# A gated RMS norm inside one fused layer on Trainium2: the row sums and the spread of the reciprocal root, by transposes instead of fp32 matmuls

## The chip, the cores and the metric

The kernel runs on one core of one Trainium2 chip. The metric is the device time of one execution in microseconds (us); the time before is 1612.79 us, the median of three runs that lie between 1611.87 and 1614.87.

Engine names are those of the profile: PE is the matrix engine's matmuls, PEld its weight loads, DVE the vector engine, ACT the scalar engine (ScalarE), POOL is GpSimd, SP the engine that only issues DMAs. "Column" below means a block of 128 sequence positions, which is what one 128 x 128 instruction handles.

## The reference, cut to what matters

The reference computes one layer: a combined input projection of x (1024 positions, width 2048), sparse attention on one half of the mixing width, a Mamba-2 (SSD) mixer on the other half, one output projection and a layer norm. The change touches the last step of the SSD mixer only, the gated norm:

```
g = (y * silu(z)).reshape(bsz, seq, G, SSD_WIDTH // G)          # G = 4 groups of 256 channels
g = g * rsqrt(mean(square(g), axis=-1, keepdims=True) + RMS_EPS)  # RMS_EPS = 1e-5
return g.reshape(bsz, seq, SSD_WIDTH) * norm_w
```

For each position and each of four groups, the mean of 256 squares is taken over the channels, and its reciprocal root multiplies those 256 channels.

## The kernel before

All large products are done in three fp32r passes: an operand is split into a rounded part (tiles `wh`, `xh`, made by ACT) and the rest (tiles `wl`, `xl`, made by DVE, now and then by POOL), and PE accumulates high x high, high x low and low x high in a `pj` bank of PSUM. The sequence is worked in two halves of 512 positions (`h`); channels lie on the partitions, positions along the row. First come the input projections, whose stream of `pj` matmuls goes on to the end of the attention and SSD work; that work is slipped in between them as tasks. Then come the output projection and the layer norm.

Nothing is issued in the order in which the Python text stands. The tasks record instructions (class `Flow`, with a table of engine costs in `Sim.cost`), and then class `Order` lays the recorded instructions out once more: it gives PE, at each point, the first block within a window of 100 whose inputs are there, and each other engine the ready instruction with the earliest due time. Each engine then runs its own queue strictly in that order and waits at the head of it. So a change of an instruction's cost or engine can shift the order of everything behind it, and slots of the pools go to other tiles. All instructions are emitted by one line, L611, so the profile's groups are told apart by tile names: `u`, `xh`, `xl`, `s` are work tiles in SBUF (freed operand slots serve as work tiles too), `sm` are small ones of four columns, `a`, `o`, `pj` are PSUM banks, `c` is the constant tile `c3` whose first third is the identity, `mhalf` holds -0.5. The letter `o` as an input is the constant `o256`, 1/256 in each partition.

The gate is the task `t_gate` (L2380 to L2442). It takes one half, one group and either one chunk pair of 256 positions (two columns) or, if the group's gates are still held in the work tiles, a whole half of 512 (four columns); `wide` says which. In the program before, all 16 gates are of two columns. Its steps:

- L2405 to L2412: multiply by the gate, square on ACT, add the two squared halves of the 256 channels (`zs`, first part: 128 partitions by 256 positions).
- L2413 to L2418: per column one fp32 matmul with the squares as weights and `o256` as the one moving column. The sum over the partitions, divided by 256, lands in one column of an `a` bank, with the positions on the partitions.
- L2420: DVE adds EPS while it moves the two columns to `sm`.
- L2423: POOL raises them to -0.5 (`pow` with `mhalf`).
- L2424 to L2427: per column one fp32 matmul with the `sm` column, broadcast along the row, as weights and the identity as moving operand, which spreads the 128 roots over all partitions, along the row.
- L2428 to L2430: DVE multiplies the two halves of the channels by norm weight and root; then the tile is stored to a scratch (`mx`, `my` in the profile) which the output projection reads.

The helper `fl.mm` issues a matmul, `fl.tr` a transpose against the identity, `fl.act` an activation, `fl.ts`, `fl.stt` and `fl.two` element-wise work.

Of the kernel before, what the change touches and what calls it, by code (L numbers as in the profile page):

```python
# [13 lines left out]
AF = mybir.ActivationFunctionType  # L14
ALU = mybir.AluOpType
# [4 lines left out]
P = 128  # L20
# [3 lines left out]
EPS = 1e-5  # L24
# [843 lines left out]
class Layer:  # L868
# [687 lines left out]
    def consts(self):  # L1556
        a, nc = self.a, self.nc
        c3 = self.const("c3", [P, 3, P])
        nc.sync.dma_start(c3, a["c3"])
        self.ident, self.tri, self.ones = c3[:, 0], c3[:, 1], c3[:, 2]  # L1560
        self.fl.ident = self.ident
        self.ps, self.pso, self.res, self.mv, self.lnB = {}, {}, {}, {}, {}
        self.cw = self.const("cw", [P, 16, 5])
        nc.sync.dma_start(self.cw, a["cw"])
        self.dn = self.const("dn", [P, 2, 8])
        nc.sync.dma_start(self.dn, a["dn"])
        self.hp = self.const("hp", [P, 2, 16])
        nc.sync.dma_start(self.hp, a["hp"].partition_broadcast(P))
        self.mhalf = self.const("mhalf", [P, 4])
        nc.gpsimd.memset(self.mhalf, -0.5)  # L1570
        self.m01 = self.const("m01", [P, 384], BF)
        nc.gpsimd.memset(self.m01, 0.0)
        nc.gpsimd.memset(self.m01[0:64, 64:128], HIDE)
        nc.gpsimd.memset(self.m01[0:64, 320:384], HIDE)
        self.zero16 = self.const("zero16", [P, 2], BF)
        nc.gpsimd.memset(self.zero16, 0.0)
        self.o256 = self.const("o256", [P, 1])
        nc.gpsimd.memset(self.o256, 1.0 / 256.0)
        self.carry = self.const("carry", [P, 16, 3])
        nc.gpsimd.memset(self.carry, 0.0)  # L1580
        self.nea = self.const("nea", [P, 16])
        for h in range(2):
            setattr(self, f"sd{h}", {k: self.const(f"{k}{h}", [P, 64]) for k in ("wsc", "dt", "ac", "ddt", "cdec")})
# [796 lines left out]
    def t_gate(self, h, g, cps, xy=None, zz=None):  # L2380

        fl, nc = self.fl, self.nc
        w = 256 * len(cps)
        cols = slice(256 * cps[0], 256 * cps[0] + w)
        held = [self.zg[h, g, j] for j in range(2)]
        wide = held[0][0] is not None
        evs = () if xy is not None else tuple(self.ev_y[h, g, cp] for cp in cps)
        yield Need("", us=(xy is None) * (1 if w == 256 else 2) + (zz is None and not wide), ev=evs + tuple(e for _, e in held))
        if wide:
            zs = [x for x, _ in held]  # L2390
            xs = [fl.new("us", [P, HALF]) for _ in range(2)]
            for j in range(2):
                fl.dma(xs[j], self.y_sc[h, g][j])
            tiles = xs + zs
            part = lambda t, j: t[j]
        else:
            if zz is None:
                zz = fl.new("us", [P, 2, 256])
                fl.dma(zz, self.zs_sc[h, g][:, :, cols].rearrange("j p s -> p j s"))
            if xy is None:  # L2400
                xy = fl.new("us", [P, 2, 256])
                fl.dma(xy, self.y_sc[h, g][:, :, cols].rearrange("j p s -> p j s"))
            xs, zs, tiles = [xy], [zz], [xy, zz]
            part = lambda t, j: t[0][:, j]
        yield Need("G", late=2500.0)  # L2405
        for x, z in zip(xs, zs):
            fl.two(x, x, z, ALU.mult)
        yield Need("A")
        for x, z in zip(xs, zs):
            fl.act(z, x, AF.Square)  # L2410
        yield Need("G")
        fl.two(part(zs, 0), part(zs, 0), part(zs, 1), ALU.add)  # L2412
        yield Need("P", a=1, sm=1)  # L2413
        sm = fl.new("sm", [P, 4])
        nq = w // P
        b = fl.new("a", [P, 512])
        for c in range(nq):
            fl.mm(b[:, c:c + 1], part(zs, 0)[:, c * P:(c + 1) * P], self.o256)  # L2418
        yield Need("V")
        fl.ts(sm[:, 0:nq], b[:, 0:nq], EPS, None, ALU.add)  # L2420
        fl.free(b)
        yield Need("G")
        nc.gpsimd.tensor_tensor(out=sm[:, 0:nq], in0=sm[:, 0:nq], in1=self.mhalf[:, 0:nq], op=ALU.pow)  # L2423
        yield Need("P", a=1)  # L2424
        b = fl.new("a", [P, 512])
        for c in range(nq):
            fl.mm(b[:, c * P:(c + 1) * P], sm[:, c:c + 1].to_broadcast([P, P]), self.ident)  # L2427
        yield Need("V")  # L2428
        for j in range(2):
            fl.stt(part(xs, j), part(xs, j), self.dn[:, 1, 2 * g + j:2 * g + j + 1], b[:, 0:w], ALU.mult, ALU.mult)  # L2430
        fl.free(b, sm)
        yield Need()
        n = self.gated[h, g] = self.gated.get((h, g), 0) + len(cps)
        if wide:
            for j in range(2):
                fl.dma(self.mixed[h][8 + 2 * g + j], xs[j])
        else:
            fl.dma(self.mixed2[h][g][:, :, cols].rearrange("j p s -> p j s"), xy)
        if n == 2:
            for j in range(2):  # L2440
                fl.signal(self.ev_mix[h, 8 + 2 * g + j])
        fl.free(*tiles)  # L2442
# [212 lines left out]
```

## Time and profile before

| what | value |
|---|---|
| median of the three runs | 1612.79 us |
| the profiled execution's own time | 1613.98 us |
| its span, first to last instruction | 1612.2 us |
| mean granted PE clock | 0.997 |
| gates | 16, the first sum at 643.8 us, the last spread at 1400.4 us |

The profile is of one execution. Busy shares are over the whole span; a group of instructions is named by what it writes and reads. "Idle before" is the idle time of an engine just before the instructions of a group, with what ended it. A matmul's duration in the profile includes its pipeline, so what a matmul costs PE is read from the distance between starts, not from its length.

### The profile page before, as it was taken

What the parts mean: (1) busy time and instruction counts of PE and PEld (TensorE: products, weight loads), DVE (VectorE), ACT (ScalarE), POOL (GpSimd) and SP (SyncE); (2) the same over time, 40 slices, a digit from 0 to 9 for tenths busy, and PEclk for the clock granted to TensorE, in tenths of its full rate; (3) what the DMA queues carried; (4) which work ended last, traced back from release to release, by engine and by line L of the source; (5) the groups of instructions that cost most, each with busy time, mean ns of one, the idle gap of its engine ahead of it and who ended that gap; (6) DMA issues with size and microseconds to landing.
All of it is one profiled execution on the core that took longest, in us unless ns stands there. A gap on an engine that the chain in (4) does not pass through costs nothing. (4 is left out here: it accounts for less than half of the span.)

```text
span 1612.2 us, 24012 instructions
## 1 busy us (share of the span) xinstructions
PE 1592.8 (99%) x7996; PEld 1338.9 (83%) x7996; DVE 1327.0 (82%) x2437; ACT 1005.9 (62%) x1774; POOL 213.3 (13%) x212
## 2 busy tenths in 40 slices
PE   9999999999999999999999999999999999999997
PEld 7888898888788888888888888888878888888885
DVE  6989999988689976879676787867888788559998
ACT  5565666758989799785443557768775754332420
POOL 0000110200101110302021313222120101000100
PEclk9999999999999999999999999999999999999999
DMA  9657956999779877687665675589899889847554
GB/s 344 218 190 259 335 182 237 340 402 379 270 239 307 298 264 239 224 302 271 211 236 179 219 229 160 158 278 294 266 298 347 287 298 358 282 151 241 183 179 131
DMA packets 192637, 414.49 MB, mean 257 GB/s; under 512 B 19712, under 2 KB 56192, under 8 KB 192512
## 3 DMA queue, kind: packets, MB, share of 16 engines
q1 hardware_dynamic: 192080, 412.56, 75.6%
q8 instruction: 63, 1.03, 0.3%
q14 instruction: 62, 0.51, 0.1%
q10 hardware_dynamic: 432, 0.39, 0.1%
HBM read 308.94 MB, written 103.94 MB: 256 GB/s over the span
## 5 line engine op out<-in xcount | busy, mean ns | idle before, releaser
L611 PE MATMUL pj<-xh,wh 128*128 128x512 f32 (+1 forms) x1496 | 581.5, 389 | 0.0
L611 PE MATMUL pj<-xh,wl 128*128 128x512 f32 (+1 forms) x1496 | 571.2, 382 | 0.1
L611 PE MATMUL pj<-xl,wh 128*128 128x512 f32 (+1 forms) x1496 | 570.8, 382 | 0.0
L611 ACT ACTIVATE wh<-wr 128x1024 fp32r<-128x1024 f32 (+2 forms) x241 | 248.8, 1033 | 210.9 <-PE pj L611 185.9
L611 DVE TENSOR_TENSOR wl<-wr,wh 128x1024 fp32r<-128x1024 f32 (+2 forms) x236 | 283.4, 1201 | 63.8 <-ACT wh L611 61.3
L611 PEld LDWEIGHTS pj<-xh,wl 128*128 128x128 f32 x1496 | 281.5, 188 | 56.1 <-DVE wl L611 0.5
L611 PEld LDWEIGHTS pj<-xh,wh 128*128 128x128 f32 x1496 | 281.6, 188 | 50.8 <-issue 1.5
L611 PEld LDWEIGHTS pj<-xl,wh 128*128 128x128 f32 x1496 | 282.0, 189 | 49.0
L611 PE MATMUL a<-u,u 128*128 128x512 f32 (+3 forms) x742 | 172.6, 345 | 0.8 <-DVE u L611 0.5
L611 DVE TENSOR_TENSOR u<-u,u 128x512 f32<-128x512 f32 (+7 forms) x208 | 135.4, 661 | 15.0 <-ACT u L611 5.0
L611 PEld LDWEIGHTS a<-u,u 128*128 128x128 f32 x742 | 124.4, 190 | 19.8 <-DVE u L611 0.9
L611 ACT ACTIVATE u<-s,sm 128x768 bf16<-128x768 f32 (+7 forms) x132 | 129.0, 978 | 11.4 <-DVE sm L611 9.4
L611 PE MATMUL pj<-wh,xh 128*128 128x512 f32 x334 | 133.9, 401 | 0.0
L611 PE MATMUL pj<-wh,xl 128*128 128x512 f32 x334 | 130.5, 391 | 0.0
L611 PE MATMUL pj<-wl,xh 128*128 128x512 f32 x334 | 130.3, 390 | 0.0
L611 DVE TENSOR_TENSOR wr<-wr,wr 128x1024 f32<-128x1024 f32 (+1 forms) x83 | 102.9, 1241 | 24.1 <-DMA wr<-wt 23.3
L611 ACT ACTIVATE u<-u 128x512 f32<-128x512 f32 (+4 forms) x147 | 81.1, 558 | 57.2 <-DVE u L611 42.5
L611 ACT ACTIVATE a<-a 128x512 f32<-128x512 f32 (+3 forms) x160 | 78.0, 504 | 54.4 <-PE a L611 52.8
L611 DVE TENSOR_TENSOR u<-pj,u 128x512 f32<-128x512 f32 (+1 forms) x112 | 74.4, 665 | 21.7 <-PE pj L611 17.8
L611 POOL TENSOR_SCALAR s<-s,sm 128x640 f32<-128x640 f32 (+7 forms) x64 | 62.8, 992 | 193.8 <-DVE sm L611 153.8
L611 ACT ACTIVATE u<-a 128x512 fp32r<-128x512 f32 (+4 forms) x114 | 52.4, 477 | 44.1 <-PE a L611 40.5
L611 ACT ACT_TABLE_LOAD x57 | 73.1, 1283 | 10.7 <-issue 5.9
(258 smaller groups left out, 2214.9 us busy)
## 6 DMA issues: line engine op xcount, KB each, us to landing
wr<-wt SPq DMA_DIRECT2D x187, 512.0 KB, 4.9
u<-u SPq DMA_DIRECT2D x110, 256.0 KB, 4.5
wr<-t SPq DMA_DIRECT2D x44, 512.0 KB, 5.2
u<-wo SPq DMA_DIRECT2D x64, 256.0 KB, 4.5
ts<-u SPq DMA_DIRECT2D x64, 256.0 KB, 4.2
wr<-ts SPq DMA_DIRECT2D x32, 512.0 KB, 4.5
s<-xt SPq DMA_DIRECT2D x25, 512.0 KB, 6.1
t<-wr SPq DMA_DIRECT2D x22, 512.0 KB, 4.9
```

Of the source, the lines that this page charges most:

```text
L611: getattr(engines[x.eng], x.op)(*[real(v) for v in x.args], **{k: real(v) for k, v in x.kw.items()})
```

## The change

The matmuls for the sum are replaced by transposes of the squares: positions come to lie on the partitions and channels along the row of a PSUM bank. ACT then reads each column's 128 x 128 block with `Identity`, a scale of 1/256 and a bias tile `eps` holding EPS/128, and its accumulator adds up the row: 128 x EPS/128 + sum/256 is the mean plus EPS. The written block goes to the second part of `zs`, which nobody reads any more. The DVE instruction that added EPS is gone. The spread is a transpose of the broadcast column in place of a matmul with the identity.

```diff
@@ consts
-        self.o256 = self.const("o256", [P, 1])
-        nc.gpsimd.memset(self.o256, 1.0 / 256.0)
+        self.eps = self.const("eps", [P, 1])
+        nc.gpsimd.memset(self.eps, EPS / 128)
@@ t_gate
         for c in range(nq):
-            fl.mm(b[:, c:c + 1], part(zs, 0)[:, c * P:(c + 1) * P], self.o256)
-        yield Need("V")
-        fl.ts(sm[:, 0:nq], b[:, 0:nq], EPS, None, ALU.add)
+            fl.tr(b[:, c * P:(c + 1) * P], part(zs, 0)[:, c * P:(c + 1) * P])
+        yield Need("A")
+        for c in range(nq):
+            fl.act(part(zs, 1)[:, c * P:(c + 1) * P], b[:, c * P:(c + 1) * P], AF.Identity, bias=self.eps, scale=1.0 / 256,
+                   accum_out=sm[:, c:c + 1])
         fl.free(b)
         yield Need("G")
         nc.gpsimd.tensor_tensor(out=sm[:, 0:nq], in0=sm[:, 0:nq], in1=self.mhalf[:, 0:nq], op=ALU.pow)
         yield Need("P", a=1)
         b = fl.new("a", [P, 512])
         for c in range(nq):
-            fl.mm(b[:, c * P:(c + 1) * P], sm[:, c:c + 1].to_broadcast([P, P]), self.ident)
+            fl.tr(b[:, c * P:(c + 1) * P], sm[:, c:c + 1].to_broadcast([P, P]))
```

The planner lays the program out anew. In the changed program there are 15 gates, 14 of two columns and one of four, so still 32 columns. The orders of the instructions differ from shortly before the first gate on; up to there they are the same.

The first place is PE's queue at the first gate, where both programs still stand alike; `a_6711` before and `a_6713` now is the bank of the sum, `u_6604` the tile of squares. Before:

```order
L611 MATMUL pj_6559<-xh_5626,wl_6570 128x512
L611 MATMUL a_6711<-o_136,u_6604 128x1 x2
L611 MATMUL a_6717<-u_6103,u_6324 128x128
L611 MATMUL a_6717<-u_6045,u_6324 128x128
L611 MATMUL a_6717<-u_6103,u_6324 128x128
```

and now:

```order
L611 MATMUL pj_6559<-xh_5626,wl_6570 128x512
L611 MATMUL a_6713<-c_318,u_6604 128x128 x2
L611 MATMUL a_6716<-u_6105,u_6328 128x128
L611 MATMUL a_6716<-u_6046,u_6328 128x128
L611 MATMUL a_6716<-u_6105,u_6328 128x128
```

The two fp32 matmuls with one moving column have become two transposes in the same place. A row of this order is an instruction as the program issues it.

The second place is the queue of the engine that takes the sum out of PSUM, at a gate in the thick of the last input projections. Before it is DVE's; `sm_12302<-a_12294` is the sum, `wl` and `wr` are weights being split or added for the stream of projections, `dt` and `ddt` scale tiles of the SSD scan:

```order
L611 TENSOR_TENSOR wl_12265<-wr_11926,wh_12254 128x1024
L611 TENSOR_TENSOR wr_12059<-wr_12059,wr_12089 128x1024
L611 TENSOR_TENSOR u_12232<-a_12277,dt_1859 128x256
L611 TENSOR_TENSOR u_12235<-a_12277,ddt_2809 128x256
L611 TENSOR_TENSOR wr_12146<-wr_12146,wr_12229 128x1024
L611 TENSOR_SCALAR sm_12302<-a_12294 128x2
L611 TENSOR_TENSOR u_11817<-u_11817,u_12107 128x512
```

Now it is ACT's; this is the gate of four columns, `sm_13030` its sums and `wh` weights being rounded:

```order
L611 ACTIVATE wh_12973<-wr_12701 128x1024
L611 ACTIVATE u_12912<-u_12912 128x512
L611 ACTIVATE wh_13010<-wr_12794 128x1024
L611 ACTIVATE u_12959<-u_12959 128x512
L611 ACTIVATE u_12354,sm_13030<-a_13021,eps 128x128 x4
L611 ACT_TABLE_LOAD
L611 ACTIVATE u_13066<-s_2425_12256 64x512 x2
```

The step has left DVE's queue, where it stood behind splits and additions of weights, for ACT's, where it stands behind roundings of weights. The number of table loads on ACT is 57 in both programs.

## The prediction

> **What bounds the kernel now.** I read the page's head first: which engine is full, and whether at full clock.
>
> ```profile
> span 1612.2 us, 24012 instructions
> PE 1592.8 (99%) x7996; PEld 1338.9 (83%) x7996; DVE 1327.0 (82%) x2437; ACT 1005.9 (62%) x1774; POOL 213.3 (13%) x212
> PEclk9999999999999999999999999999999999999999
> ```
>
> PE is busy 1592.8 of 1612.2 us. Only 19.4 us are idle, so what PE no longer has to issue comes off the end, unless a new wait takes its place. The view of waits says what PE waited for:
>
> ```profile
> PE a L611 <- POOL sm L611: 2.9, 1, 2.9
> PE a L611 <- DVE u L611: 2.1, 3, 0.8
> ```
>
> The longest wait belongs to the gate itself: one spread matmul, reading `sm` from POOL, came 2.9 us late. The table by stages shows where the gates stand (640 to 1400 us) and what else is loaded there:
>
> ```profile
> 640.00:900.00 260.00, 259.44 (x1408) 222.25 (x1407) 202.37 (x421) 150.03 (x279) 52.63 (x42) 1.00 0.70 236
> 900.00:1100.00 200.00, 199.08 (x1069) 169.74 (x1067) 155.86 (x301) 137.84 (x259) 57.76 (x69) 1.00 0.67 215
> 1100.00:1400.00 300.00, 296.90 (x1587) 247.85 (x1586) 239.10 (x408) 188.63 (x309) 38.27 (x32) 0.99 0.92 309
> 1560.00:1613.00 53.00, 40.92 (x181) 33.57 (x179) 46.21 (x76) 0.00 (x0) 3.92 (x4) 0.94 0.39 125
> ```
>
> The columns are length, busy PE, PEld, DVE, ACT and POOL, granted clock, DMA share, GB/s. In the three gate stages ACT is busy 150, 138 and 189 us of 260, 200 and 300 (58, 69 and 63%), DVE 78, 78 and 80%. PE is the bound; ACT has the most room of the engines that feed it.
>
> **The change part by part.** First, what PE issues. The groups of the gate's matmuls, and of the transposes that the kernel has elsewhere:
>
> ```profile
> L611 PE MATMUL a<-c,s 128*128 128x128 f32 x288 | 42.1, 272 | 0.0
> L611 PE MATMUL a<-c,sm 128*128 128x128 f32 x64 | 10.1, 281 | 3.1 <-POOL sm L611 2.9
> L611 PE MATMUL a<-o,u 128*128 128x1 f32 x52 | 6.6, 231 | 0.0
> L611 PE MATMUL a<-o,xh 128*128 128x1 f32 x8 | 1.0, 229 | 0.0
> L611 PE MATMUL a<-o,s 128*128 128x1 f32 x4 | 0.5, 228 | 0.0
> ```
>
> The program issues 32 sums and 32 spreads, but the trace has 64 of each (52 + 8 + 4, and 64): an fp32 matmul runs as two passes. The transposes, mostly `a<-c,s`, stand as often in the trace as the program issues them, 408 in all: one pass each. So 64 passes of 128 go.
>
> What a pass costs is in the distance between starts. PE's timeline at one sum, at one spread and at one pair of transposes, each between projections:
>
> ```profile
> 1315.09 0.50 PE L611 MATMUL a<-o,xh 128*128 128x1 f32 x4
> 1315.45 0.48 PE L611 MATMUL pj<-wh,xh 128*128 128x512 f32 x1
> 1315.77 0.39 PE L611 MATMUL pj<-wl,xh 128*128 128x512 f32 x1
> 1316.00 0.39 PE L611 MATMUL pj<-wh,xl 128*128 128x512 f32 x1
> ```
> ```profile
> 1321.35 0.61 PE L611 MATMUL a<-c,sm 128*128 128x128 f32 x4
> 1321.71 0.48 PE L611 MATMUL pj<-wh,xh 128*128 128x512 f32 x1
> 1322.03 0.39 PE L611 MATMUL pj<-wl,xh 128*128 128x512 f32 x1
> ```
> ```profile
> 773.51 0.38 PE L611 MATMUL a<-c,s 128*128 128x128 f32 x2
> 773.65 0.48 PE L611 MATMUL pj<-xh,wh 128*128 128x512 f32 x1
> 773.96 0.40 PE L611 MATMUL pj<-xl,wh 128*128 128x512 f32 x1
> ```
>
> A projection matmul starts 0.23 us after the one before it (1315.77 to 1316.00), but the first one behind a small block takes 0.32: part of the cost of the block falls on its follower, so I count to the start of the second follower. The sum: 1315.77 - 1315.09 = 0.68, less one projection step of 0.23, is 0.45 us. The spread: 1322.03 - 1321.35 = 0.68, again 0.45. Two transposes: 773.96 - 773.51 = 0.45, less 0.23, is 0.22. Each block saves 0.23 us; two blocks at each of 16 gates make 32 x 0.23 = 7.4 us. That one gate now has four columns changes nothing, since 32 columns stay. By busy time instead, 64 + 64 passes take 6.6 + 1.0 + 0.5 + 10.1 = 18.2 us and 64 transposes 64 x 42.1/288 = 9.4, which saves 8.8; but these lengths overlap, so I take 7.4.
>
> Second, the step that takes the sum out of PSUM. DVE did it in one short instruction, and POOL's power waits for it. At the gate with the long wait, DVE's timeline and then POOL's:
>
> ```profile
> 1165.71 1.22 DVE L611 TENSOR_TENSOR wr<-wr,wr 128x1024 f32<-128x1024 f32 x1
> ...
> 1167.51 1.21 DVE L611 TENSOR_TENSOR wr<-wr,wr 128x1024 f32<-128x1024 f32 x1
> 1168.65 0.15 DVE L611 TENSOR_SCALAR sm<-a 128x2 f32<-128x2 f32 x1
> 1168.72 1.28 DVE L611 TENSOR_TENSOR u<-u,u 128x512 f32<-128x512 f32 x2
> ```
> ```profile
> 1168.87 2.82 POOL L611 TENSOR_TENSOR sm<-sm,mhalf 128x2 f32<-128x2 f32 x1 [19.31 <-DVE sm L611]
> ```
>
> The small step stood behind additions of weights until 1168.65, and then the power took 2.82 us beside two-input work on DVE, against a median of 718 ns:
>
> ```profile
> L611 POOL TENSOR_TENSOR sm<-sm,mhalf x16: 688/718/2817, 644.6 to 1398.0; 128x2 f32<-128x2 f32 x16
> L611 DVE TENSOR_SCALAR sm<-a x16: 148/153/159, 644.3 to 1397.7; 128x2 f32<-128x2 f32 x16
> ```
>
> The change takes 16 x 0.15 = 2.5 us off DVE, which is beside PE's work and counts nothing by itself, and takes the step out of that queue: 2.9 us of PE's waiting was there. The Trainium skill, SBUF — State Buffer, section "SBUF: two separate sides", has DVE and GpSimd exclude each other for a whole instruction on a shared port pair; the 2.82 us agree, and by that rule the power stays as exposed as before, since it stays on POOL.
>
> Third, what ACT gets: 32 activations of 128 x 128 from PSUM, each with a read of the accumulator. No row has just this form; the nearest are:
>
> ```profile
> L611 ACT ACTIVATE wh<-wr 128x1024 fp32r<-128x1024 f32 x232 | 244.6, 1054 | 208.6 <-PE pj L611 185.9 <-issue 21.1 <-ACT a L611 1.1
> L611 ACT ACTIVATE s<-s,ac 128x128 f32<-128x128 f32 x128 | 40.9, 390 | 0.4
> L611 ACT ACTIVATION_READ_ACCUMULATOR s<-s,sm 128x1 f32 x64 | 12.1, 189 | 0.0
> L611 ACT ACTIVATE u<-a 128x128 f32<-128x128 f32 x28 | 7.4, 265 | 8.6 <-PE a L611 8.6
> ```
>
> Between 265 (from PSUM, no bias tile) and 390 + 189 = 579 ns each (with a bias tile, from SBUF, nothing overlapped); I take 0.45, so 0.9 us per gate of two columns and 32 x 0.45 = 14.4 us over 760 us of gate stages in which ACT idles some 280. Hidden, then; what is not hidden is the longer chain. It goes transpose 0.27 (the 272 ns above), ACT 0.9, power 0.72, with handovers about 2.0 us, where it was 0.27 + 0.15 + 0.72, about 1.2. What covers it is the work that PE has between a gate's two blocks. Counted in the changed order with 0.23 us per 512-wide matmul, that is at least 3.0 us: four gates have 2.9 to 3.2, the others 3.5 to 16.7. So 0.9 us is left at those four for ACT's queue. One rounding of weights (1054 ns) ahead costs 0.15, two cost 1.2. New waits at the four gates are thus 0 to 4 x 1.2 = 4.8 us; with nothing to decide I take half, 2.4.
>
> The sum against the profiled execution: 1613.98 - 7.4 (passes) - 2.9 (the wait for POOL) + 2.4 (new waits on ACT) = 1606.1. The median of the runs is 1.2 below the profiled execution's own time, so 1604.9 us for the median, which is the forecast.
>
> **Rivals.** *The chain stays hidden everywhere.* Then no new waits: 1612.8 - 10.3 = 1602.5. For it: ACT's idle time and a cover that is above 2.0 us at all gates. Against: the order is new in most of the gate stages, and PE's other waits, 2.1 us on DVE `u`, fall anew; if they went too it would be 1600.4.
>
> *The gate's wait is paid back.* The power meets a busy DVE at one close gate (2.82 - 0.72 = 2.1 us) and ACT's queue costs 4.8, and the 2.9 goes: 1612.8 - 10.3 + 6.9 = 1609.4, or 1610 with small change: no difference worth the name. For it: three of 16 gates were late in reaching their spread before. Against: it needs all four close gates.
>
> *Slower: POOL's power decides.* It still needs DVE's pauses, now with 0.8 us less cover. If four gates waited 2.9 us each, as one did, that is 11.6 - 7.4, 4.2 us more: 1617. It decides from 7.4 / 2.9 = three such gates on. Against: just one of 16 did, at the most crowded DVE queue of the region.
>
> *The transposes are no cheaper than the matmuls*, run in two passes with an fp32 operand broadcast along the row: 1612.8. Against: the 408 transposes with one pass each. None of them has a broadcast operand, though.
>
> *The clock falls.* In the last stage, where PE is busy for 40.92 of 53 us, the granted clock was 0.94. At that clock the 760 us of gate stages would take 6% more: 1612.8 + 46 - 7 = 1651. Against: the kernel runs 408 transposes already at a granted clock of 1.00, 1.00 and 0.99 in those stages, and the followers of the pair at 773.51 are back at 0.23 to 0.24 us. This is the rule that speaks against the change: the Trainium skill, TensorE: Matmul & The Clock Gate, "Part 4: PE-mode transpose", says that transposes do not count as busy time for the clock gate. If the 64 were enough to shut it, this would be the price; the 408 were not.
>
> **How the numbers follow.** Forecast 0.63; chain hidden 0.20; paid back 0.10; POOL decides 0.04; no cheaper 0.02; clock 0.01. The range reaches from 1600.6, where the hidden chain's best case stands, to 1609.8, just past the paid-back case, and leaves out a little of the first two and the last three cases. A difference of 0.2% (3.2 us) is about what a measurement can tell from none: below 1609.6 is faster. Forecast and hidden chain give 0.83; same 0.12 (paid back and no cheaper); slower 0.05.
>
> **What would show it.** In the profile after: `a<-o` groups gone, `a<-c,sm` with 32 instead of 64, and PE's total of instructions lower by 64; the steps between starts around a pair 0.45 us from the first transpose to the second follower. DVE without the 16 `sm<-a`; ACT with 32 new accumulator reads, 0.27 to 0.58 us a column. PE's view of waits with POOL `sm` under 2.4 us in all. The prediction is wrong if the passes don't come off PE's busy time, if the waits of PE outside the gates grow by more than 3 us, or if the clock of a gate stage is below 0.99.

## The result and the profile after

The changed kernel takes 1602.11 us (median of four runs, 1600.85 to 1603.55) against 1613.83 for the kernel before in the same session: a ratio of 0.9925, with a 95% interval of 0.991 to 0.994. In a second session on another chip it was 1600.48 against 1612.05, 0.993 (0.9915 to 0.9944). The forecast was 1604.9; 1602.1 is in the range and near the rival in which the chain stays hidden, at 1602.5.

The profiled execution took 1600.85 us. The head of its page:

```profile
span 1599.1 us, 23973 instructions
PE 1583.2 (99%) x7932; PEld 1329.9 (83%) x7932; DVE 1321.9 (83%) x2418; ACT 1016.4 (64%) x1838; POOL 218.5 (14%) x211
```

PE has 7932 instructions, exactly 64 fewer, and its busy time is 9.6 us shorter. Its idle time, span less busy, is 15.9 us instead of 19.4. So of 13.1 us in the spans, 9.6 are work or its spacing, and 3.5 are waits. PE's waits after:

```profile
PE pj L611 <- DVE u L611: 1.8, 2, 1.3
PE a L611 <- POOL s L611: 1.4, 1, 1.4
PE a L611 <- DVE u L611: 0.9, 2, 0.5
PE a L611 <- POOL sm L611: 0.4, 1, 0.4
```

The wait at the gate, `a` on POOL `sm`, has gone from 2.9 to 0.4 us. The waits on DVE `u` have moved to other places and are 2.7 in all.

The groups of the spread, matmul (PE) and weight load (PEld); then the weight load that there was in its place before (the matmuls before, 64, stand in the prediction):

```profile
L611 PE MATMUL a<-c,sm 128*128 128x128 f32 x32 | 6.0, 273 | 0.4 <-POOL sm L611 0.4
L611 PEld LDWEIGHTS a<-c,sm 128*128 128x128 f32 x32 | 4.2, 135 | 2.6 <-POOL sm L611 0.9
```
```profile
L611 PEld LDWEIGHTS a<-c,sm 128*128 128x128 f32 x64 | 9.2, 189 | 5.4 <-POOL sm L611 4.4 <-issue 0.2
```

32 instead of 64: the broadcast column is transposed in one pass like any other tile. The load of its weights takes 135 ns, and took 189 for each pass before. PE's timeline at one pair:

```profile
1286.59 0.38 PE L611 MATMUL a<-c,sm 128*128 128x128 f32 x2
1286.73 0.48 PE L611 MATMUL pj<-wh,xh 128*128 128x512 f32 x1
1287.04 0.40 PE L611 MATMUL pj<-wl,xh 128*128 128x512 f32 x1
```

From the first transpose to the second follower 0.45 us pass, the number that the prediction read from another pair; less one projection step of 0.23 this is 0.22 for the block, where it was 0.45.

What ACT got is seen best at the one gate where PE still waited. The sums' transposes on PE, then ACT's timeline, POOL's, and PE's at the spread:

```profile
1301.18 0.38 PE L611 MATMUL a<-c,u 128*128 128x128 f32 x2
```
```profile
1302.07 1.06 ACT L611 ACTIVATE s<-s 128x1024 f32<-128x1024 f32 x1
1303.04 0.35 ACT L611 ACTIVATE u<-a,eps 128x128 f32<-128x128 f32 x1
1303.28 0.19 ACT L611 ACTIVATION_READ_ACCUMULATOR u<-a,eps 128x1 f32 x1
1303.38 0.35 ACT L611 ACTIVATE u<-a,eps 128x128 f32<-128x128 f32 x1
1303.63 0.20 ACT L611 ACTIVATION_READ_ACCUMULATOR u<-a,eps 128x1 f32 x1
```
```profile
1303.90 1.25 POOL L611 TENSOR_TENSOR sm<-sm,mhalf 128x2 f32<-128x2 f32 x1 [2.81 <-ACT u L611]
```
```profile
1305.20 0.43 PE L611 MATMUL a<-c,sm 128*128 128x128 f32 x2 [0.45 <-POOL sm L611]
```

Two columns take ACT 0.79 us from the first activation to the end of the second read (1303.63 + 0.20 - 1303.04), with the handover to POOL 0.86; the prediction had 0.9. A read of the accumulator begins 0.1 us before its activation ends, so a column costs about 0.34 us of ACT's time and not the sum of the two rows.

Two delays meet at this gate. The transposes ended at 1301.56 (1301.18 + 0.38), but ACT was in other work and took the sums only at 1303.04, 1.48 us later; and the power took 1.25 us where its median before was 0.72, 0.53 more. PE's wait of 0.45 us is less than either, so by these numbers it needed both. At ten of the 15 gates ACT came to the sums straight from other work, with no idle time; at all gates but this one, PE had enough work ahead of the spread to cover that.

### The profile page after: what moved, and what is told of

It is laid out like the page before. It is cut to its first block, busy times and chain, and to the rows that moved or that the text cites. A ratio compares the mean times of both kernels' runs of the same rounds, so it can differ in the third digit from the quotient of the medians.

```text
span 1599.1 us, 23973 instructions
## 1 busy us (share of the span) xinstructions
PE 1583.2 (99%) x7932; PEld 1329.9 (83%) x7932; DVE 1321.9 (83%) x2418; ACT 1016.4 (64%) x1838; POOL 218.5 (14%) x211
## 4 chain that ended last, share of the span: by engine, by line
PE 84%; DMA 6%; DVE 5%; ACT 2%; issue 1%; SPq 0%; POOL 0%; DVEq 0%; ACTq 0%; POOLq 0%
PE pj L611 67%; PE a L611 14%; PE o L611 3%; DMA wr<-wt 3%; DVE u L611 2%; DMA u<-u 1%; DVE s L611 1%; ACT u L611 1%; DVE wl L611 1%; DMA wr<-t 1%; DVE wr L611 0%; DMA z<-u 0%; DMA t<-wr 0%; DVE xl L611 0%; DMA u<-o 0%
## 5 line engine op out<-in xcount | busy, mean ns | idle before, releaser
L611 DVE TENSOR_TENSOR u<-u,u 128x512 f32<-128x512 f32 (+7 forms) x202 | 130.7, 659 | 13.1 <-DMA u<-wo 5.3
L611 DVE SCALAR_TENSOR_TENSOR s<-a,wsc,s 128x512 f32<-128x512 f32 (+3 forms) x120 | 74.1, 644 | 5.2 <-ACT a L611 5.0
```

Source lines behind the costliest of these rows:

```text
L611: getattr(engines[x.eng], x.op)(*[real(v) for v in x.args], **{k: real(v) for k, v in x.kw.items()})
```

## The experiments

Two theories were to be told apart. *Passes*: PE is the bound, so 64 passes of 0.11 us come off the end. *Order*: the planner lays out a new order whenever a cost changes, and the waits and spacings of that order make the difference; the passes matter little.

### With the order held

In two kernels only what is emitted changes: the plan, and so every queue's order, is that of the kernel before or of the changed one, and the spread instruction alone is exchanged. In a third each sum transpose is issued twice. The diff shows only the lines that emit; the 32 instructions get their mark `swap` where `t_gate` records them.

```diff
 # e3_before_order: plan with matmuls, emit transposes
+            if getattr(x, "swap", False):
+                self.nc.tensor.transpose(*[real(v) for v in x.args])
+                continue
 # e4_after_order: plan with transposes, emit matmuls
+            if getattr(x, "swap", False):
+                self.nc.tensor.matmul(*[real(v) for v in x.args], start=True, stop=True)
+                continue
 # e5_sum_twice: the sum transposes are marked, and emitted once more
+            if getattr(x, "swap", False):
+                self.nc.tensor.transpose(*[real(v) for v in x.args])
```

> The program before, in its own order row for row, with only the 32 spread matmuls emitted as transposes. Theory (a pass removed from PE comes off the end): 32 passes of 0.112 us go, 3.6 us less than before, so about 1610.2 against 1613.8, and the one wait of 2.9 us of PE on POOL sm stays in the view of waits. Rival (the gain came from the new order and from waits that it removed, the passes were hidden): within 1 us of before.

Measured: 1611.68 us against 1613.81, 0.9985 (0.9976 to 0.9995), a gain of 2.1 where 3.6 was expected. The head of its page and the longest wait of PE:

```profile
span 1609.2 us, 23948 instructions
PE 1588.1 (99%) x7964; PEld 1333.5 (83%) x7964; DVE 1322.1 (82%) x2437; ACT 1007.1 (63%) x1774; POOL 216.4 (13%) x212
```
```profile
PE a L612 <- POOL sm L614: 5.3, 3, 2.6
```

The passes are gone, 7964 instructions, and PE's busy time is 4.7 us shorter. But the wait at the gates has grown from 2.9 to 5.3 us, in three places where there was one, against the expectation; the old one is still 2.6. At the largest of the new ones PE is ready 0.6 us earlier than before and the power starts 0.9 us later. All of PE's idle time together is 21.1 us, 1.7 more than before, and the span is 3.0 shorter. So in this execution part of the saved time turned into waiting. The runs' times alone do not show it: their interval allows gains of 0.8 to 3.9 us, which holds the 3.6 of the passes and, at its edge, the rival's 1.

> The changed program, in its own order row for row, with only the 32 spread transposes emitted as fp32 matmuls again. Theory (passes): 3.6 us more than the changed program, 1605.7. Rival (order and waits made the gain): within 1 us of 1602.1.

Measured: 1604.36, ratio to before 0.9939 (0.9926 to 0.9953), 2.3 us above the changed kernel's 1602.11, which ran in another session. In the profiles:

```profile
span 1601.5 us, 24037 instructions
PE 1586.7 (99%) x7964; PEld 1334.2 (83%) x7964; DVE 1325.7 (83%) x2418; ACT 1017.0 (64%) x1838; POOL 222.4 (14%) x211
```

> The changed program in its own order, with each of the 32 sum transposes issued twice in a row into the same place of the bank. Theory (a transpose costs PE one pass of 0.11 us and nothing hides it): 3.5 us more than the changed program, 1605.6. Rival (a transpose is hidden beside the projections' stream): within 1 us of 1602.1.

Measured: 1604.04, ratio to before 0.9939 (0.9926 to 0.9953); span 1601.6, PE busy 1586.7 in 7964 instructions. Both have 3.5 us more PE work than the changed kernel (1586.7 - 1583.2), as 32 passes of 0.11 should. The times alone do not decide between the theories: by the ratios, 0.9939 against 0.9925 for the changed kernel, both are 2.3 us longer, between the rival's 1 and the theory's 3.5, and the intervals overlap. The spans can be held against two profiled executions of the changed program (the second is e12_after_again, below), whose busy time is the same. Against the first they are 2.4 and 2.5 longer, with 1.1 and 1.0 us less idle time; against the second, 3.4 and 3.5 longer at like idle time. So the passes are in PE's work in full, and the idle time of one order moves by 1 us from execution to execution. That added work fills waits is not shown.

### With the instructions held

Here the program before keeps PE's instructions, and the planner's table has another cost, so for PE only the order differs. With the order a few things change beside PE: some element-wise work goes from DVE to POOL or back, and ACT loads tables 67 times in e6_order_a, 55 in e7_order_b and 63 in e11_pow_before, where it was 57.

```diff
 # e6_order_a, e7_order_b (Sim.cost, fp32 matmul of up to 8 columns)
-... if n > 8 else 226.0
+... if n > 8 else 111.0     # e7: 200.0
 # e11_pow_before (Sim.cost, small tensor_tensor on POOL)
-            t = 180 + 2.16 * n if n > 8 else 600 + 120 * n
+            t = 180 + 2.16 * n if n > 8 else 1400 + 120 * n
```

> The program before with the same instructions, but planned as if a sum matmul took 111 ns in place of 226, so only the order differs, from shortly before the first gate on. Theory (the order alone moves a few us by the waits that happen to fall, in either direction, and PE's instructions set the rest): PE has 7996 instructions as before, and the time lies within 4 us of 1613.8, the difference being that of PE's waits. Rival (planning the gates cheaper is what brought the gain): about 1606 or below, with no pass removed.

Measured: 1606.56 against 1613.81, 0.996 (0.9946 to 0.9974): 7.2 us from the order alone, with what the planner moved along with it. That is outside the 4 us of the first theory and about where its rival put it. The page's head:

```profile
span 1605.0 us, 24058 instructions
PE 1590.0 (99%) x7996; PEld 1338.3 (83%) x7996; DVE 1327.8 (83%) x2440; ACT 1018.0 (63%) x1784; POOL 210.4 (13%) x209
```

All 7996 instructions are there; PE's idle time is 15.0 instead of 19.4 us, and no wait on POOL `sm` is left in the view of waits, though DVE still moves the sums. Busy time is 2.8 lower too, with the same instructions: a matmul that starts late while the one before it still runs counts as busy. Which starts these were is not taken apart here.

> The program before with the same instructions, planned as if a sum matmul took 200 ns in place of 226: a second order, new only from about 640 us on. If the order moves the time by the waits that happen to fall, this one falls anywhere within 8 us of before, 1606 to 1618, with PE's idle time and the time moving by the same amount; if planning the sums cheaper brings the gain of the first such order by a rule, it lies at 1610 or above, since 200 is nearly 226.

Measured: 1610.32 against 1614.28, 0.997 (0.9958 to 0.9981); PE's idle time 16.9 us. The number lies inside the one reading and at the edge of the other, so it does not part them by itself. But 26 ns less in the table bring 4.0 us where 115 less bring 7.2, which is no proportion. Idle time moves with the time once more, though not by the same amount as expected: 2.5 us of 3.7 in the span.

> The program before with the same instructions, planned as if POOL's power took 800 ns more. If the wait at the gates was worth its 3 us, PE's waits on POOL sm go and the time is 3 us less than before, give or take 4 for the other waits of the new order; 7996 PE instructions stay.

Measured: 1608.40 against 1612.05, 0.9978 (0.9968 to 0.9987), 3.7 us; the wait on POOL `sm` is down to 0.2 and idle to 15.8 us. As expected: put later by the planner, the spreads no longer wait. Here a step was planned dearer and the time fell too, so a cheaper plan is not the rule behind the gain. All three redrawn orders were faster than the program's own; whether its own was an unlucky one, three cannot tell.

### One part of the change at a time, planned as such

```diff
 # e8_evac_act: the program before, sums moved by ACT
-        yield Need("V")
-        fl.ts(sm[:, 0:nq], b[:, 0:nq], EPS, None, ALU.add)
+        yield Need("A")
+        fl.act(sm[:, 0:nq], b[:, 0:nq], AF.Identity, bias=self.eps)   # eps holds EPS
 # Order: fp32 matmuls of one column are blocks of their own
-            x.full = ... and kind_of(x.ins[1]) == "float32"
+            x.full = ... and kind_of(x.ins[1]) == "float32" and x.n > 1
 # e1_spread_only: the program before with
-            fl.mm(b[:, c * P:(c + 1) * P], sm[:, c:c + 1].to_broadcast([P, P]), self.ident)
+            fl.tr(b[:, c * P:(c + 1) * P], sm[:, c:c + 1].to_broadcast([P, P]))
 # e2_sum_only: the changed program with that spread line as it was before
```

> The program before with its fp32 matmuls, but the two sums of a gate go from PSUM to the small tile by one ACT activation that adds EPS, and not by DVE. Theory (the step waited in DVE's queue, and POOL's power and PE's spread behind it): PE's waits on POOL sm fall from 3 us to under 1, with 7996 PE instructions; the time 3 us less than before, give or take 4 for the new order. Rival (the waits came from POOL's power beside DVE's work and not from the queue): POOL sm waits of 2 us or more stay.

Measured: 1612.74 against 1614.28, 0.999 (0.998 to 0.9999), 1.5 us. PE's waits that matter here:

```profile
PE o L611 <- DVE u L611: 1.8, 1, 1.8
...
PE pj L611 <- ACT wh L611: 1.2, 1, 1.2
PE a L611 <- POOL sm L611: 1.1, 1, 1.1
```

The wait on POOL `sm` falls to 1.1, between what the two theories said, and the time lies within the theory's range, but the order is new here as well, not least because the planner's blocks are divided otherwise. Others, on ACT's weights and on DVE `u`, have come in its place, and PE's idle time is 18.5.

> Only the spread by transposes, planned so; the sums stay fp32 matmuls that DVE takes out. Theory (passes and waits): 7964 PE instructions, 3.5 us less PE work, and the rest is whatever waits the new order has: 1610 less or more by up to 4. Rival (the change of the sum makes all of the gain): as before, 1612 to 1615.

Measured: 1606.20 against 1614.28, 0.995 (0.9935 to 0.9964), 8.1 us; 7964 instructions, idle 17.0. The rival's 1612 to 1615 is excluded, and the theory's range of 1606 to 1614 holds the time at its very end. The wait on POOL `sm` is down to 0.7 us, with the sums still on DVE.

> Only the sum by transposes and ACT, planned so; the spread stays a pair of fp32 matmuls. Theory: 7964 PE instructions, 3.5 us less PE work and no DVE queue ahead of the power, 1607 less or more by up to 4. Rival (the spread makes all of the gain): as before, 1612 to 1615.

Measured: 1608.06 against 1614.28, 0.9959 (0.9944 to 0.9974), 6.2 us; 7964 instructions, idle 18.2. Here, too, the rival is excluded. PE's longest wait, and one of its three places: the sums' transposes on PE, then ACT's, POOL's and PE's timelines:

```profile
PE a L611 <- POOL sm L611: 2.9, 3, 1.4
```
```profile
1244.49 0.38 PE L611 MATMUL a<-c,u 128*128 128x128 f32 x2
...
1244.81 1.28 ACT L611 ACT_TABLE_LOAD   x1
1246.10 0.63 ACT L611 ACTIVATE u<-u 128x512 f32<-128x512 f32 x1
1246.64 0.26 ACT L611 ACTIVATE u<-a 128x128 f32<-128x128 f32 x1
1246.80 0.36 ACT L611 ACTIVATE u<-a,eps 128x128 f32<-128x128 f32 x1
...
1247.67 0.90 POOL L611 TENSOR_TENSOR sm<-sm,mhalf 128x2 f32<-128x2 f32 x1 [3.53 <-ACT u L611]
...
1248.63 0.71 PE L611 MATMUL a<-c,sm 128*128 128x128 f32 x4 [1.01 <-POOL sm L611]
```

With the step on ACT, PE waits 2.9 us for POOL `sm` again, but in three other places. At the one shown the transposes ended at 1244.87, and ACT, behind a table load and two activations, took the sums at 1246.80, 1.93 us later; PE waited 1.01. At a second (0.47 us of waiting) the sums stood 3.8 us before ACT took them. At the third (1.42 us) ACT was quick, and the power stood in POOL's own queue behind a 128x512 element-wise instruction that waited for a DMA. So one queue's wait has gone and other queues' waits have come.

### The changed program in other orders

```diff
 # e9_margin: the changed program with
-    MARGIN = 500.0
+    MARGIN = 1000.0
 # e10_pow_after: the changed program with the cost of e11_pow_before
```

> The changed program, planned with a margin of 1000 ns in place of 500 before PE is given a block, so that a late input is covered by more work. If PE's remaining waits (4 us of its starts) come from inputs a little later than planned, 1 to 3 us less than the changed program, about 1600; if the order moves the time by chance, within 5 us of 1602 on either side.

Measured: 1602.82 against 1612.05, 0.9946 (0.993 to 0.9962), and not better than the changed program's 1600.48 in the same session; the intervals overlap. Its profiled execution, the slowest of its four, took 1606.06 us:

```profile
span 1604.3 us, 23962 instructions
PE 1584.9 (99%) x7932; PEld 1329.5 (83%) x7932; DVE 1317.7 (82%) x2418; ACT 1013.5 (63%) x1838; POOL 210.9 (13%) x211
```

> The changed program, planned as if POOL's power took 800 ns more, so that each spread is put later. The wait for POOL sm was 0.4 us, so little is to be had from it: PE's wait on POOL sm goes, and the time is the changed program's, less or more by what the other waits of the new order make, up to 4 us.

Measured: 1599.91 against 1612.05, 0.9927 (0.9913 to 0.9942); PE waits no longer on POOL `sm`, idle 14.8 us. It cannot be told from the changed program.

> The changed program itself, beside the others on the same chip: 0.9925 of before, as its first runs gave, within 0.0015.

Measured: 0.993 (0.9915 to 0.9944), as told above; span 1598.1, PE busy 1583.2, idle 14.9.

### Put together

The profiled executions, one of each kernel and two of the changed one, by the number of PE's instructions and their idle time:

| PE instructions | idle near 15 us | idle near 17 us | idle near 19 us |
|---|---|---|---|
| 7996 | e6_order_a: 15.0, span 1605.0; e11_pow_before: 15.8, 1606.7 | e7_order_b: 16.9, 1608.5 | before: 19.4, 1612.2; e8_evac_act: 18.5, 1611.2 |
| 7964 | e4_after_order: 14.8, 1601.5; e5_sum_twice: 14.9, 1601.6 | e1_spread_only: 17.0, 1604.5 | e2_sum_only: 18.2, 1607.1 |
| 7932 | again: 14.9, 1598.1; e10_pow_after: 14.8, 1598.2; after: 15.9, 1599.1 | none | e9_margin: 19.4, 1604.3 |

Left out is e3_before_order, with 7964 instructions and 21.1 us of idle time in 1609.2. At like idle time the spans differ by busy time, so the table says what the passes do to PE's busy time. In the first column 32 passes are worth 3.5 and 3.4 us (1605.0, 1601.5, 1598.1), in the second 4.0 (1608.5 to 1604.5). 64 passes are worth 6.9 and 7.6 in the first column (1605.0 to 1598.1 and 1606.7 to 1599.1), and 7.9 in the last (1612.2 to 1604.3). By their starts they should be 64 x 0.11 = 7.0. Along the first row the same PE instructions cost 7.2 us more or less by the order.

So of the 13.1 us between the first two profiles, about 7 are passes and about 6 are the new order's fewer waits and better spacing; this is an estimate from single executions, and the kernel before alone took 1609.88 to 1616.55 us within one session. Of the 6, 3.5 us are idle time. The rest is within PE's busy time; the changed program had the same 1583.2 in both its profiles, so that is hardly chance from run to run, but which starts it came from stays open.

## Why the prediction held, point by point

- *The passes, 7.4 us.* Right: 64 instructions less, 0.22 us per block where it was 0.45, and 6.9 to 7.9 us at like idle time. Not foreseen: where the old order was held, PE's busy time fell by 4.7 us and its idle time took 1.7 of them back (e3_before_order, one execution).
- *The wait for POOL, 2.9 us.* The size was right (2.9 to 0.4), the reason was not enough, so that the term came out is in part luck. The wait was said to leave with the step's departure from DVE's queue. But it also leaves, or nearly, with the step on DVE in other orders (none in e6_order_a, 0.2 in e11_pow_before, 0.7 in e1_spread_only), and with the step on ACT there can be as much of it at other gates (e2_sum_only). So leaving DVE's queue is neither needed nor enough. What decides, as far as these runs show, is the order: how much work PE has ahead of the spread, and what stands ahead of the sum and the power in the queues that take them.
- *New waits on ACT, 2.4 us, half of a bound.* The mechanism was there, the size was not: 0.4 us at one gate, where the sums stood 1.48 us before ACT took them and the power was slow. The chain's part on ACT was sized rightly (0.86 for 0.9). ACT was not free when the sums came, at ten of 15 gates, but PE's work covered that at all but one. In e2_sum_only, with other work ahead of the spreads, it did not. With 0.4 in place of 2.4, the sum gives 1613.98 - 7.4 - 2.9 + 0.4 = 1604.1 for the profiled execution, which took 1600.85.
- *The other waits.* They were a remark beside a rival and not a term. They were among what the remaining 3.2 us came from: the idle time fell by 3.5 us in all, of which 2.5 at the gates, and busy time fell by 9.6 where the passes account for 7.4. So for the profiled execution the sum, 1606.1, missed by 5.3 us: 2.0 for waits on ACT that did not come and 3.2 for the better order, which had no term. That the medians differ by only 2.8 (1604.9 and 1602.1) is luck: the execution profiled before was 1.2 us above its median, and the one profiled after 1.3 below.
- *The rivals.* The chain stayed hidden, or nearly, and that rival's 1602.5 is the nearest number. The transposes with a broadcast operand were as cheap as others. The power did meet a busy DVE (1.25 us at the gate shown), but at one close gate. The price of the rival in which POOL decides was too high: the 2.9 us of the gate that waited before were in the 1612.8 already, so four such gates would have added 8.7 and not 11.6, which makes 1614 and not 1617. The granted clock of the profiled execution is 0.997 as before, so what the Trainium skill, TensorE: Matmul & The Clock Gate, "Part 4: PE-mode transpose", says of transposes and the gate did not show here with 64 more of them.

## What to carry to other kernels

Where PE is 99% busy, count its hardware passes: an fp32 matmul against a one-column or an identity operand is two, a transpose one, and here the difference came off the end, give or take what the waits did. But when a planner orders the work, any change of a cost is also a draw of a new order: here the same PE instructions spread over 7 us, as much as the 64 passes were worth. So run the change with the order held, and the order with the instructions held, before the gain is put down to the edit.

## What was not expected of the hardware

The read of the accumulator overlaps the activation before it: two columns with their reads, listed at 0.35 and 0.19 us each, followed each other at 0.34 us (1303.04 to 1303.38). Beside a plain activation this is still dear: in the rows of e2_sum_only above, the plain `u<-a` of the same shape is followed after 0.16 us (1246.64 to 1246.80). And weight loads differ by what the matmul is: 189 ns for a pass of the fp32 matmul that spread the roots, 135 for the transpose of the same broadcast column.
